# Layer 1's input projection in eight pairs over both streams, seven block products for each pair

## The chip, the cores and the metric

The program runs on one core of a Trainium2 chip, in one launch. The metric is the device time of one execution in microseconds (us). Six queues of instructions matter: TensorE (PE in the rows; its weight loads are PEld), VectorE (DVE), ScalarE (ACT), GpSimd (POOL), and SyncE (SP) and ACT also issue DMAs. Each engine executes its own instructions in order and waits on semaphores for the others.

## The reference

A two-layer encoder trunk is applied to two requests ("streams") with the same weights, each of 512 tokens and 1024 channels. What the change touches is the first matmul of a layer and what reads it:

```python
h = _rmsnorm(x, norm_mix)
proj = h @ w_in
q, k, v, g, hy_in, pool_in = jnp.split(proj, [R, 2 * R, 3 * R, 4 * R, 4 * R + 3 * HY_WIDTH], axis=-1)
ret = _head_layernorm(_retention(_rope(q) * dk ** -0.5, _rope(k), v, ...), ret_gn) * silu(g)
hy_out = _hyena(hy_in, hy_short_conv, ...)      # conv of width 3, two long convolutions by FFT
pool_out = _pool_mixer(pool_in, pool_w, pool_scale)
x = x + concat([ret, hy_out, pool_out]) @ w_out
```

`w_in` has 1024 rows and 3072 columns: 512 each for q, k, v and g (four heads of 128), 768 for the Hyena group, 256 for the pooling group. After it come a gated MLP with 2816 hidden channels and a gated per-layer embedding. All arithmetic is held to float32 accuracy.

## The kernel before

**Layout.** Activations are stored transposed: a tile holds 128 channels by 512 tokens of one stream. A weight tile of the projection is 128 output columns by all 1024 input channels, that is eight blocks of 128x128. The names of the tiles are q0 to q3, k0 to k3, g0 to g3 (one for each head), hy0 to hy5, pl0 and pl1; v stands apart, as v00 to v11, because it is computed with the tokens on the partitions (`values`).

**Float32 from float16.** Each operand is split into a high and a low float16 part (`split`: ACT writes the high part, DVE or POOL the low one), and each 128x128 block takes three matmuls: high with high, high with low, low with high. So one tile of one stream is 8 x 3 = 24 matmuls of 512 columns (`mm3`). Raw weights are loaded by SP into four buffers (`wraw`), scaled and split into nine buffers (`wspl`); both streams use a split tile while it lasts.

**Normalised input.** `norm_steps` sums squares with a small matmul (cs), DVE and POOL turn it into a scale, and eight small matmuls broadcast that into a PSUM tile (rb). `h_steps` then makes eight tiles h: DVE multiplies (hn), ACT casts the high part, and the low part is a subtraction, on DVE for the even tiles and on POOL for the odd ones.

**Pairs in the MLP.** From its fourth pair of weight tiles on, the MLP already works on both streams at once (`ffn_joint`): two weight tiles, cut into two halves of their input channels, are a 2 x 2 block matrix, the two halves of h of the two streams are another, and their product is formed with seven block products instead of eight (the form of Strassen and Winograd). Each block product (`product`) is 4 x 3 = 12 matmuls. The right-hand operands are four blocks of h and four sums of them (`ffn_sums`: 16 tiles hs, made from the kept float32 tiles hn of both streams by 16 subtractions, ten of them on POOL, and 16 splits). The left-hand operands are sums of weight blocks (`piece_pair`: four subtractions on POOL, then four splits). The results come out in three PSUM banks X, Y and Z and are combined by ACT copies (r) and DVE additions. `lace` interleaves the seven products of a pair with those of the next.

**Order of the work.** PE and SP follow exactly the order in which the program emits instructions. That order comes from a small planner (`schedule`): the work is cut into Python generators ("threads": one main thread for each stream, and threads for retention heads, Hyena, pooling, filters), each step states how long it occupies PE and how long its result will take, and the planner runs whatever is ready, side threads first. The first stream's main thread may run ahead of the second by a few weight tiles (`LAG`). The order on DVE, ACT and POOL is set by the framework's scheduler. In layer 1 of the version before, stream 0 does v, then q0, k0, g0, hy0 and so on; stream 1 follows some 40 us later through the same tiles, and the steps of heads (sc, ov), Hyena (tp, sp, iv) and pooling (pq) of both streams lie between them. The projection of the mixing output (o0 to o7) follows.

## Time and profile before

| | |
|---|---|
| median of 3 runs | 2470.57 us (2466.92 to 2471.66) |
| the profiled execution | 2464.75 us, of which its span, first to last instruction, is 2463.0 us |
| PE busy | 2387.3 us, 97% of the span |
| DVE, ACT, POOL busy | 1778.7, 1034.5 and 715.4 us (72%, 42%, 29%) |
| mean granted TensorE clock | 0.989 of full speed |
| layer 1's mixing, from the second stream's rb to the first MLP tile | 1304 to 1720 us of the span |

The busy share tells which engine sets the pace on average; the rows of waits tell where PE, although busiest, had to stand still. The time of a stretch in which PE is always busy is the number of its matmuls times their spacing. [...]

### The profile page before, as it was taken

How to read it: one execution, taken by the hardware profiler on the slowest of the kernel's cores; microseconds unless marked ns; L12 is line 12 of the kernel's file. 1: busy time of each engine (PE TensorE's matmuls, PEld its weight loads, DVE VectorE, ACT ScalarE, POOL GpSimd, SP SyncE). 2: the span in 40 equal slices, each digit the busy share in tenths (PEclk: the TensorE clock that was granted, in tenths of full speed). 3: DMA queues.
4: the chain of work that ended last, by engine and by line, in shares of the span. 5: the costliest groups of instructions: out<-in, count | busy, mean ns of one | idle time of the engine just before them, and what ended most of it. 6: DMA issues, size and time to landing. Idle time of an engine off the chain costs nothing.

```text
span 2463.0 us, 30876 instructions
## 1 busy us (share of the span) xinstructions
PE 2387.3 (97%) x12024; PEld 1171.1 (48%) x12024; DVE 1778.7 (72%) x2520; ACT 1034.5 (42%) x1555; POOL 715.4 (29%) x534
## 2 busy tenths in 40 slices
PE   5999989999999999999999999999999999999997
PEld 3544654444444444444456555544444444444443
DVE  7984886868877868866575686464987786976655
ACT  5543334344534435444533343332553453544441
POOL 3222343124234233320121223520423424332011
PEclk9999999999999999999999999999999999999998
DMA  6121020330121121113232111131012112111301
GB/s 225 65 97 62 25 75 8 128 132 32 50 68 54 52 69 48 60 53 114 73 123 91 67 43 52 35 115 64 25 46 68 57 47 69 54 58 52 112 1 69
DMA packets 64363, 168.60 MB, mean 68 GB/s; under 512 B 7574, under 2 KB 13718, under 8 KB 64216
## 3 DMA queue, kind: packets, MB, share of 16 engines
q1 hardware_dynamic: 58312, 156.40, 19.2%
q10 hardware_dynamic: 5904, 10.23, 1.1%
q8 instruction: 94, 1.54, 0.3%
q14 instruction: 53, 0.43, 0.1%
HBM read 152.18 MB, written 14.42 MB: 68 GB/s over the span
## 4 chain that ended last, share of the span: by engine, by line
PE 74%; DVE 16%; issue 4%; ACT 3%; POOL 1%; DMA 1%; SPq 0%; ACTq 0%; POOLq 0%; DVEq 0%
PE fx L1169 13%; PE ex L1169 7%; PE fy L1169 7%; PE ey L1169 4%; PE fz L1169 3%; DVE wspl L171 2%; PE s L326 2%; PE s L327 2%; PE s L328 2%; PE ez L1169 2%; DVE t L174 2%; DVE conv L171 2%; PE o L327 2%; PE o L328 2%; PE o L326 2%
## 5 line engine op out<-in xcount | busy, mean ns | idle before, releaser
L1169 PEld LDWEIGHTS <-wspl 128*128 128x128 f16 x4704 | 461.1, 98 | 566.1 <-issue 13.9
L174 POOL TENSOR_TENSOR wraw<-wraw 128x512 f32<-128x512 f32 (+1 forms) x240 | 345.5, 1440 | 653.6 <-DVE wspl L171 639.5
L168 ACT ACTIVATE wspl<-wraw 128x1024 f16<-128x1024 f32 (+2 forms) x360 | 327.1, 910 | 381.6 <-POOL wraw L174 71.1
L171 DVE SCALAR_TENSOR_TENSOR wspl<-wraw,wspl 128x1024 f16<-128x1024 f32 (+2 forms) x354 | 387.7, 1096 | 84.8 <-ACT wspl L168 83.6
L1169 PE MATMUL fx<-hs,wspl 128*128 128x512 f16 x1368 | 312.3, 382 | 7.6 <-ACT r L168 7.6
L326 PEld LDWEIGHTS <-wspl 128*128 128x128 f16 x1536 | 152.3, 99 | 182.0 <-issue 8.6
L328 PEld LDWEIGHTS <-wspl 128*128 128x128 f16 x1536 | 150.7, 98 | 183.8 <-issue 4.1
L327 PEld LDWEIGHTS <-wspl 128*128 128x128 f16 x1536 | 150.7, 98 | 177.9 <-issue 4.8
L1169 PE MATMUL ex<-at,wspl 128*128 128x512 f16 x846 | 192.7, 379 | 0.0
L174 POOL TENSOR_TENSOR y<-t,mhalf 128x4 f32<-128x4 f32 x30 | 36.1, 1203 | 399.6 <-DVE t L178 388.8
L168 ACT ACTIVATE at<-conv 128x512 f16<-128x512 f32 x142 | 89.3, 629 | 145.5 <-DVE conv L174 110.8
L174 DVE TENSOR_TENSOR at<-conv,at 128x512 f16<-128x512 f32 x142 | 126.0, 888 | 26.9 <-ACT at L168 25.5
L171 DVE SCALAR_TENSOR_TENSOR conv<-r,scaled,conv 128x511 f32<-128x511 f32 x152 | 130.5, 859 | 2.1 <-ACT conv L168 0.4
L1169 PE MATMUL fx<-h,wspl 128*128 128x512 f16 x456 | 104.6, 379 | 0.0
L1169 PE MATMUL fy<-h,wspl 128*128 128x512 f16 x456 | 104.6, 379 | 0.0
L1169 PE MATMUL fy<-hs,wspl 128*128 128x512 f16 x456 | 104.6, 379 | 0.0
L1169 PE MATMUL fz<-h,wspl 128*128 128x512 f16 x456 | 104.6, 379 | 0.0
L168 ACT ACTIVATE conv<-conv 128x512 f32<-128x512 f32 x88 | 55.3, 629 | 109.5 <-DVE conv L171 108.4
L1169 PE MATMUL ey<-at,wspl 128*128 128x512 f16 x432 | 101.1, 379 | 0.0
L174 DVE TENSOR_TENSOR acc<-acc,sq 128x512 f32<-128x512 f32 x84 | 64.2, 766 | 49.7 <-ACT sq L168 48.6
L168 ACT ACTIVATE sq<-x 128x512 f32<-128x512 f32 x80 | 49.5, 624 | 117.1 <-DVE x L171 58.5
L328 PE MATMUL s<-xs,wspl 128*128 128x512 f16 x256 | 97.0, 379 | 0.0
(246 smaller groups left out, 4758.7 us busy)
## 6 DMA issues: line engine op xcount, KB each, us to landing
wraw<-in_w SPq DMA_DIRECT2D x172, 512.0 KB, 3.7
wraw<-in_w SPq DMA_DIRECT2D x48, 384.0 KB, 3.0
x<-in_x SPq DMA_DIRECT2D x32, 256.0 KB, 4.7
dec<-ddec SPq DMA_DIRECT2D x16, 448.0 KB, 4.6
wraw<-in_w SPq DMA_DIRECT2D x16, 256.0 KB, 2.6
xsp<-x ACTq DMA_DIRECT2D x16, 256.0 KB, 2.1
x<-xsp SPq DMA_DIRECT2D x16, 256.0 KB, 4.7
out_y<-out SPq DMA_DIRECT2D x16, 256.0 KB, 2.8
```

The source lines that it names most:

```text
L168: return self.nc.scalar.activation(out=out, in_=in_, func=func, **k)
L171: return self.nc.vector.scalar_tensor_tensor(out=out, in0=in0, scalar=scalar, in1=in1, op0=op0, op1=op1)
L174: return (eng or self.nc.vector).tensor_tensor(out=out, in0=in0, in1=in1, op=op)
L326: self.nc.tensor.matmul(out, wv[:, 0, kb, :], x[:, 0], start=first, stop=False)
L327: self.nc.tensor.matmul(out, wv[:, 0, kb, :], x[:, 1], start=False, stop=False)
L328: self.nc.tensor.matmul(out, wv[:, 1, kb, :], x[:, 0], start=False, stop=last)
L1169: mm = lambda a, b, start=False, stop=False: self.nc.tensor.matmul(out, a, b, start=start, stop=stop, skip_group_check=not first)
```

## The change

In layer 1 only (`TWINNED`), 16 of the 20 tiles q, k, g, hy and pl are taken as eight pairs (`TWINS`): q0 with k0, hy0 with g0, hy1 with hy2, hy3 with q1, k1 with g1, hy4 with q2, k2 with hy5, g2 with pl0. Each pair is computed for both streams together with seven block products (`mix_joint`), steps m0.0 to m7.6. The remaining four, pl1, q3, k3 and g3, follow for each stream by itself. `h_steps` keeps the float32 tiles, and `ffn_sums` makes the 16 sums when the second stream's h is there. The first stream's thread, after its v tiles, waits until the joint part is done; the second one, after its own v tiles, runs it. What follows each tile (rotation, convolution, gate, and the start of head, Hyena and pooling threads) is moved into `take`, which is called with the right stream when a result is complete. Layer 0 is as before. The core of the diff:

```diff
+TWINS = (("q0", "k0"), ("hy0", "g0"), ("hy1", "hy2"), ("hy3", "q1"), ("k1", "g1"), ("hy4", "q2"), ("k2", "hy5"), ("g2", "pl0"))
+TWINNED = (1,)
...
+        steps[4:4] = lace([f"m{i}" for i in range(len(TWINS))])
...
-            yield from self.h_steps(s, x, acc, vec[:, V_NMIX:V_NMIX + NB], h)
+            M = self.mix[l]
+            yield from self.h_steps(s, x, acc, vec[:, V_NMIX:V_NMIX + NB], h, M.hn[s] if l in TWINNED else None)
             x = None
+            M.h[s] = h
+            if s == 1 and l in TWINNED:
+                self.ffn_sums(M)
...
+                if l in TWINNED and not M.done.owner and s == 1:
+                    M.done.owner = self
+                    yield [self.decay_ev[l]]
+                    yield from self.mix_joint(l, M)
+                    M.done.set(self.clock)
+                    yield 0.0, 0.0
+                elif l in TWINNED and M.done.time is None:
+                    yield [M.done]
...
+            p = st["XYZXYXX"[q]]
+            self.product(p, w, right[q], q < 3)
+            i, s, box = 0, 0, []
+            if q in (0, 1, 3):
+                r = st[("r1", "r5", None, "r2")[q]] = self.g(name="r")
+                self.act(r, p)
+                r = None
+            elif q == 6:
+                i, box = 1, [p]
+                del state[key]
+            else:
+                n = {2: "r1", 4: "r2", 5: "r5"}[q]
+                self.tt(st[n], p, st[n], ALU.add)
+                i, s, box = int(q == 5), int(q > 2), [st.pop(n)]
+                if q < 5:
+                    del st["Z" if q == 2 else "Y"]
```

In the emitted PE order, nothing differs up to the second stream's rb of layer 1, nor from the second stream's first MLP tile on. Behind the joint part, the seven-product chain of the last pair ends with its sixth and seventh product in a row, both into bank X, with a DVE addition that reads X after the sixth.

PE, right behind the second stream's rb in layer 1. Before, the first stream's q0 follows (it reads h of the first stream, made 20 us earlier):

```order
L751 LDWEIGHTS rr2_10734
L751 MATMUL rb_10861<-identr_91,rr2_10734 128x128
L326 LDWEIGHTS wspl_10737
L326 MATMUL q0_10914<-h_10488,wspl_10737 128x512 [waits Activation_49]
L327 LDWEIGHTS wspl_10737
```

Now the second stream's v tiles follow (vp), which read the h tiles (h_10862 and on) that are made from this very rb:

```order
L762 LDWEIGHTS rr2_10734
L762 MATMUL rb_10851<-identr_91,rr2_10734 128x128
L342 LDWEIGHTS h_10862 [waits Activation_49]
L342 MATMUL vp_10964<-wspl_10230,h_10862 128x256
L343 LDWEIGHTS h_10862
L343 MATMUL vp_10964<-wspl_10230,h_10862 128x256
L344 LDWEIGHTS h_10862 [waits DVE_49]
L344 MATMUL vp_10964<-wspl_10230,h_10862 128x256
L342 LDWEIGHTS h_10867 [waits Activation_49]
```

The two tiles of q0 and k0 that stood between rb and the second stream's v are gone from there; four blocks of v now stand in a row.

POOL at the same place. Before, the second stream's four low parts of h follow one another:

```order
L174 TENSOR_TENSOR h<-hn,h 128x512 x4
L174 TENSOR_TENSOR y<-t,mhalf 128x4
L174 TENSOR_TENSOR h<-hn,h 128x512 x4
L174 TENSOR_TENSOR sw<-sw,rope 128x512
L174 TENSOR_TENSOR rt<-rt,sw 128x512
```

Now the subtractions for the sums (hn<-hn) are mixed in:

```order
L185 TENSOR_TENSOR h<-hn,h 128x512 x4
L185 TENSOR_TENSOR y<-t,mhalf 128x4
L185 TENSOR_TENSOR hn<-hn 128x512
L185 TENSOR_TENSOR h<-hn,h 128x512
L185 TENSOR_TENSOR hn<-hn 128x512
L185 TENSOR_TENSOR h<-hn,h 128x512
L185 TENSOR_TENSOR hn<-hn 128x512 x2
L185 TENSOR_TENSOR h<-hn,h 128x512
L185 TENSOR_TENSOR hn<-hn 128x512 x3
L185 TENSOR_TENSOR h<-hn,h 128x512
L185 TENSOR_TENSOR hn<-hn 128x512 x3
```

Behind y, the last low part of h (tile 7) moved from fourth to eleventh place; seven subtractions stand ahead of it.

DVE, in the first stream's Hyena step between the inverse transform (iv, on PE) and the next transposes (tp, on PE, which read abs). Before:

```order
L171 SCALAR_TENSOR_TENSOR conv_11793<-hy0_11768,scaled1_192,conv_11793 128x511 [waits DVE_49]
L174 TENSOR_TENSOR rt_11830<-k1_11797,rope_10910 128x512 [waits PE_49,Activation_49]
L174 TENSOR_TENSOR qk_11834<-rt_11830,qk_11834 128x512 [waits Activation_49]
L171 SCALAR_TENSOR_TENSOR yv_11864<-iv_11837,qs_11862 128x256 [waits Activation_49]
L171 SCALAR_TENSOR_TENSOR yv_11864<-iv_11837,qs_11862 128x256
L174 TENSOR_TENSOR yv_11864<-yv_11864,conv_11477 128x512 [waits DVE_49]
```

Now:

```order
L185 TENSOR_TENSOR r_12141<-my_11970,r_12141 128x512 [waits Activation_49]
L182 SCALAR_TENSOR_TENSOR conv_12125<-mx_11508,scaled1_192,conv_12125 128x511 [waits DVE_49]
L182 SCALAR_TENSOR_TENSOR conv_12159<-r_12141,scaled1_192,conv_12159 128x511 [waits Activation_49]
L185 TENSOR_TENSOR r_11983<-mx_11765,r_11983 128x512 [waits PE_49]
L182 SCALAR_TENSOR_TENSOR conv_12159<-r_12141,scaled1_192,conv_12159 128x511 [waits DVE_49]
L182 SCALAR_TENSOR_TENSOR wspl_12433<-wraw_11623,wspl_12433 128x1024 [waits Activation_49]
L182 SCALAR_TENSOR_TENSOR yv_12190<-iv_12163,qs_12188 128x256 [waits DVE_49]
L182 SCALAR_TENSOR_TENSOR yv_12190<-iv_12163,qs_12188 128x256
L185 TENSOR_TENSOR yv_12190<-yv_12190,conv_12125 128x512 [waits DVE_49]
```

The addition r_11983 reads bank X of the pair hy3, q1 after its sixth product, which PE executes behind iv and two more products; it now stands ahead of the reading of iv. For the second stream's iv it is the addition after the third product of the pair k1, g1.

## Rows read from the trace of the kernel before

**Rows 1.** The page, busy time by engine: busy us (share of the span), instructions.
```profile
PE 2387.3 (97%) x12024; PEld 1171.1 (48%) x12024; DVE 1778.7 (72%) x2520; ACT 1034.5 (42%) x1555; POOL 715.4 (29%) x534
```
**Rows 2.** Windows, layer 1's mixing: length, busy us of each engine, granted clock, DMA share, GB/s.
```profile
1304.00:1720.00 416.00, 413.66 (x2335) 223.51 (x2333) 259.18 (x403) 152.16 (x232) 112.92 (x95) 1.00 0.20 69
```
**Rows 3.** PE's waits in the same stretch: us in total, times, longest.
```profile
PE cs L741 <- ACT sq L168: 2.3, 2, 1.7
```
**Rows 4.** Timeline of PE, second stream's rb: start us, duration us, instruction [idle before].
```profile
1303.70 0.61 PE L751 MATMUL rb<-identr,rr 128*128 128x128 f16 x8
1304.14 0.38 PE L326 MATMUL q<-h,wspl 128*128 128x512 f16 x1
1314.50 0.27 PE L331 MATMUL vp<-wspl,h 128*128 128x256 f16 x1
1319.74 0.38 PE L326 MATMUL g<-h,wspl 128*128 128x512 f16 x1
```
**Rows 5.** Timeline of POOL there: the second stream's first and last low part of h.
```profile
1308.42 1.16 POOL L174 TENSOR_TENSOR h<-hn,h 128x512 f16<-128x512 f32 x1 [13.78 <-ACT h L168]
...
1314.55 1.15 POOL L174 TENSOR_TENSOR h<-hn,h 128x512 f16<-128x512 f32 x1 [1.01 <-ACT h L168]
```
**Rows 6.** Timeline of POOL, second stream, MLP of layer 1: subtractions mixed with low parts.
```profile
1739.63 1.27 POOL L174 TENSOR_TENSOR hn<-hn 128x512 f32<-128x512 f32 x1 [9.44 <-DVE hn L171]
...
1751.09 5.06 POOL L174 TENSOR_TENSOR hn<-hn 128x512 f32<-128x512 f32 x3
1756.11 1.60 POOL L174 TENSOR_TENSOR h<-hn,h 128x512 f16<-128x512 f32 x1
```
**Rows 7.** Timeline of PE there: rb, and the MLP tile that reads h.
```profile
1736.17 0.61 PE L751 MATMUL rb<-identr,rr 128*128 128x128 f16 x8
...
1757.76 0.38 PE L327 MATMUL fg<-h,wspl 128*128 128x512 f16 x1 [0.69 <-POOL h L174]
```
**Rows 8.** Windows behind idle stretches of PE (columns as in rows 2).
```profile
626.50:630.80 4.30, 4.23 (x12) 1.60 (x12) 3.85 (x5) 1.63 (x4) 2.40 (x2) 0.60 0.00 0
47.50:54.00 6.50, 6.44 (x31) 5.10 (x32) 6.27 (x15) 2.70 (x4) 1.39 (x1) 0.51 0.76 258
...
1283.00:1286.20 3.20, 3.20 (x17) 2.25 (x17) 2.47 (x5) 1.11 (x2) 0.00 (x0) 0.52 0.98 354
```
**Rows 9.** Timeline of PE: the wait ahead of the first, and two shorter waits.
```profile
626.57 3.74 PE L1169 MATMUL fx<-hs,wspl 128*128 128x512 f16 x10 [3.83 <-ACT r L168]
...
1282.89 0.40 PE L333 MATMUL vp<-wspl,h 128*128 128x256 f16 x1 [1.36 <-POOL h L174]
...
1617.96 1.05 PE L741 MATMUL cs<-ones,sq 128*128 128x1 f32 x8 [1.71 <-ACT sq L168]
```
**Rows 10.** DVE groups of 1300 to 1660: busy us, mean ns of one, idle before.
```profile
L171 DVE SCALAR_TENSOR_TENSOR wspl<-wraw,wspl 128x1024 f16<-128x1024 f32 x24 | 30.0, 1250 | 16.4 <-ACT wspl L168 16.2
L171 DVE SCALAR_TENSOR_TENSOR conv<-hy,scaled,conv 128x511 f32<-128x511 f32 x24 | 17.9, 745 | 10.5 <-ACT conv L168 10.3
```
**Rows 11.** Tile r in the MLP of layer 1: one addition, duration min/median/max ns.
```profile
L174 DVE TENSOR_TENSOR r<-fz,r x1: 683/683/683, 1794.8 to 1794.8; 128x512 f32<-128x512 f32 x1
```
**Rows 12.** Timeline of DVE: first and last step between an iv and its tp.
```profile
1410.95 0.74 DVE L171 SCALAR_TENSOR_TENSOR yv<-iv,qs 128x256 f32<-128x256 f32 x2
...
1417.60 0.69 DVE L174 TENSOR_TENSOR abs<-ab,abs 128x512 f16<-128x512 f32 x1 [0.16 <-ACT abs L168]
```
**Rows 13.** Timeline of PE there: what follows that iv, and the tp.
```profile
1410.25 0.38 PE L331 MATMUL sc<-qk 128*128 128x512 f16 x1
...
1423.20 1.06 PE L602 MATMUL tp<-ident,abs 128*128 128x128 f16 x16
```
**Rows 14.** Timeline of PE: sc and ov of the stage's last head.
```profile
1628.81 0.38 PE L331 MATMUL sc<-qk 128*128 128x512 f16 x1
...
1637.03 0.38 PE L331 MATMUL ov<-pt,v 128*128 128x512 f16 x1
```
**Rows 15.** Timeline of DVE: the last pt of that head.
```profile
1635.34 0.69 DVE L174 TENSOR_TENSOR pt<-st,pt 128x512 f16<-128x512 f32 x1 [0.16 <-ACT pt L168]
```

More of the change, by code (lines that the diff above doesn't have):

```diff
@@ L121, in tile_order @@
     more = ["p0", "p1"] + [f"s{m}" for m in range(NB)]
-    return tiles + more, steps + more
+    return tiles + more, steps + more, mixing
 def step_time(name):
@@ L926, in main_thread @@
-            h = None
+                box = [self._proj(l, name, h, s)]
+                yield from self.take(l, s, name, box, M, 5.15)
+            h = M.h[s] = None
             if s == 1:
                 self.rope = None
+            mix, done = M.mix[s], M.ends[s]
             yield done
@@ L1025, in main_thread, with take @@
             nc.sync.dma_start(out=io["y"][s, m], in_=t)
+    def take(self, l, s, name, box, M, cost):
+        nc, io = self.nc, self.io
+        p = box.pop()
+        if name[:2] == "hy":
+            if not M.loaded:
+                M.loaded = True
+                self.load_dft(l)
+            j = int(name[2])
+            M.hy[s][j] = self.conv3(p, self.hcw[l], j, 6)
+            p = None
+            yield cost, 0.0
+            M.hev[s][j].set(self.clock + 3.0)
+            if j == 0:
+                M.ends[s].append(Event())
+                self.spawn(self.hyena_thread(l, M.hy[s], M.hev[s], M.mix[s], M.ends[s][-1]))
+        elif name[:2] == "pl":
+            b = int(name[2])
+            if b == 0:
+                M.pw[s] = self.g(name="poolw")
+                self.load(M.pw[s][:, 0:256], io["poolw"][l])
+            rc = self.g(name="rc")
+            self.load(rc, io["rcnt"][b])
+            m = self.pooling(p, b, rc)
+            rc = p = None
+            yield cost, 0.0
+            M.ends[s].append(Event())
+            self.spawn(self.pool_thread(l, b, m, None, M.pw[s][:, b * 128:(b + 1) * 128], M.mix[s], M.ends[s][-1]))
+        elif name[0] in "qk":
+            M.qk[s].setdefault(int(name[1]), {})[name[0]] = self.rotate(p)
+            p = None
+            yield cost, 0.0
+        else:
+            hd = int(name[1])
+            sg = self.g(name="sg")
+            self.act(sg, p, ACTF.Sigmoid, scale=1.0 / WS)
+            self.stt(sg, p, 1.0 / WS, sg, ALU.mult, ALU.mult)
+            p = None
+            if hd == 0 and self.decay_ev[l].time is None:
+                yield [self.decay_ev[l]]
+            dec = self.dp.tile([128, 896], F32, tag="dec", name="dec")
+            nc.sync.dma_start(out=dec, in_=self.ddec[l, hd])
+            yield cost, 0.0
+            M.ends[s].append(Event())
+            self.spawn(self.head_thread(l, hd, M.qk[s].pop(hd), M.v[s], sg, dec, M.mix[s], M.ends[s][-1]))
@@ new lines, in mix_joint @@
+    def mix_joint(self, l, M):
+        right = self.rights(M)
+        state = {}
+        self.load_rope()
+        for _, name in STEPS[STEP_AT[l, "m0.0"]:STEP_AT[l, f"m{len(TWINS) - 1}.6"] + 1]:
+            key, q = name.split(".")
+            q = int(q)
+            w = self.weight(l, name, 0, 1)
+            st = state.setdefault(key, {})
+            if q in (0, 1, 2):
+                st["XYZ"[q]] = self.bank(name="m" + "xyz"[q])
+            p = st["XYZXYXX"[q]]
[8 more added lines that the diff above has]
+                del state[key]
+            else:
+                n = {2: "r1", 4: "r2", 5: "r5"}[q]
[3 more added lines that the diff above has]
+                    del st["Z" if q == 2 else "Y"]
+            st = p = None
+            if box:
+                yield from self.take(l, s, TWINS[int(key[1:])][i], box, M, 2.58)
+            else:
+                yield 2.58, 0.0
@@ L1229, in run @@
         self.ffn = [Ffn() for _ in range(self.depth)]
+        self.mix = [Mix() for _ in range(self.depth)]
         a = self.spawn(self.main_thread(0))
@@ L1252, in run, with __init__ @@
         self.schedule([a, b])
+class Mix:
+    def __init__(self):
+        self.h, self.hn, self.sums = [None, None], [[], []], None
+        self.mix = [[None] * NB for _ in range(2)]
+        self.hy, self.v, self.ends, self.qk, self.pw = [[None] * 6 for _ in range(2)], [[], []], [[], []], [{}, {}], [None, None]
+        self.hev = [[Event() for _ in range(6)] for _ in range(2)]
+        self.done, self.loaded = Event(), False
 class Ffn:
```

103 lines of the change are left out of this document (34 added, 69 removed).

## The prediction

> **What bounds the kernel now.** I read the page's busy times first. PE works in 97% of the span, and no other engine is above 72% [rows 1]. Then the stretch that the change touches, 1304 to 1720 us: PE is busy for 413.7 of 416 us, at the full granted clock, while DVE is busy for 259.2 (62%), ACT for 152.2 and POOL for 112.9 [rows 2]. PE's waits there come to 2.3 us in two places [rows 3]. So this stretch is as long as its matmuls. Fewer matmuls shorten it one for one, as long as PE gets its operands in time; and there is hardly any idle time to win beside them. The question is which new waits PE gets.
>
> The sum is made against the profiled execution's span of 2463.0 us. Its device time of 2464.75 us lies 5.8 us under the median of 2470.57 us; I add the difference to the median.
>
> **The matmuls.** In the timeline q0 and k0, 48 matmuls of 512 columns, take from 1304.14 to 1314.50 us [rows 4], so one takes 0.2158 us. A pair had 2 tiles x 2 streams x 24 = 96 of them and has 7 x 12 = 84 now. Eight pairs save 96 matmuls: **-20.7 us**. All of it lies on PE's path.
>
> **The second stream's v behind its own rb.** Before, q0 and k0 of the first stream stood between rb and v: rb ends at 1304.31 (1303.70 + 0.61), v starts at 1314.50 [rows 4], POOL finishes the last low part of h at 1315.70 [rows 5], and v, which walks the eight tiles in order for its first half, never waited. Now v is next to rb, and no other work of PE is put there: the first stream waits for the joint part, and its head, Hyena and pooling threads don't exist yet. So PE waits for tile 7 of h, whatever that costs. Besides, POOL now has seven subtractions for the sums ahead of that tile's low part.
>
> The same mixture exists in the MLP, where the second stream's sums are made: rb ends at 1736.78 (1736.17 + 0.61) [rows 7], POOL starts on the first subtraction at 1739.63, three subtractions in a row take 5.06 us, and the last low part ends at 1757.71 [rows 6]. That is 20.9 us behind rb. PE had other tiles to do there and still waited 0.69 us [rows 7]. With 20.9 us, tile 7 is ready at 1325.2. Of a v block (5.24 us [rows 4]) the last matmul of the first half (0.11) and the whole second half (2.62) are left then, so the block ends at 1327.95 instead of 1309.38: **+18.6 us**. The lower bound is the row without sums, 1315.70 [rows 5]: the block would end at 1318.45, +9.1. I take the upper row, because its sequence of eleven POOL operations is the one that stands here now; DVE is also busy in that time, with hn, the low parts and the first sums.
>
> POOL's low part took 1.16 us where no sums were made [rows 5] and 1.60 us amid them, and its subtraction grew from 1.27 to 1.69 us (5.06 / 3) [rows 6]. [...]
>
> With POOL at its undisturbed 1.16 and 1.27 us throughout, the eleven operations (four low parts, seven subtractions) would need 13.5 us; begun 4 us behind rb, they would end at 1321.8, and the wait would be 15.2 us.
>
> The other sums hide: the 16 low parts on DVE and 16 casts on ACT fall under the three remaining v blocks and the first products, 15.7 + 2.6 us behind the wait; the first product that reads a sum is the second of m0.
>
> **The clock behind that wait.** [...] At the start, after a longer stop, 6.44 us of work ran at 0.51 [rows 8], a loss of 3.2 us. Here PE stands for about 4 us and then does three matmuls for each tile that arrives. I take **+2.5 us**, between 1.7 and 3.2.
>
> **The end of the joint part.** The last pair's sixth and seventh product write bank X in a row, and DVE must read X in between: a matmul's tail beyond its spacing (0.38 - 0.22 [rows 4]), the addition of 0.68 [rows 11] and two hand-overs: **+1.0 us**, and up to 2.7 if the clock falls after it.
>
> **The last head.** Behind it the second stream's last head has sc, one pooling matmul, rb and then ov, about 3.9 us from the start of sc to ov; before it was 8.2 us (1628.81 to 1637.03 [rows 14]), and the last pt was done at 1636.03 [rows 15], 7.2 us after the start of sc. ov needs that pt for its last quarter, 1.9 us in; 7.2 - 5.8 is about **+1.2 us**. The wait of cs on ACT's square, 1.71 us [rows 9] of the 2.3 [rows 3], hung on the order before; those 2.3 us are taken off (**-2.3**), and **+1.0** is put in for such waits in the new order (0 to 2.3).
>
> **Hyena between iv and tp.** Both streams now pass through Hyena side by side. From iv to the last abs DVE took from 1410.95 to 1418.29, 7.3 us with one foreign instruction of 0.6 in it [rows 12], and PE came to tp 12.95 us behind iv's end (1410.25 to 1423.20 [rows 13]). Now the first stream's tp comes 13.45 us behind iv's end (an rb, two products, the other stream's iv, one product: 0.44 + 5.18 + 5.24 + 2.59). But DVE has the addition of m3's sixth product ahead of it, which is ready 5.6 us behind iv. From there: addition 0.68 [rows 11], convolution 0.75, a weight's low part 1.25 [rows 10], then 6.7 and one rotation 0.7, that is 15.7 us: 2.2 us late. For the second stream it is the addition of m4's third product, 6.1 us behind iv; then 0.68, 1.25, a low part of 0.69 [rows 12] and 6.7 + 1.4, that is 16.8 against 13.9 us: 2.9 us late. Together **+5.1 us**. No row shows this wait itself, so its bounds are 0 (if ACT or the scheduler's order gives DVE time earlier; a gain is excluded, since PE doesn't wait at these places now) and 8 (each of some 15 instructions stretched by 0.2 beside POOL's weight sums). A wait of 1.36 us [rows 9] was followed by 3.2 us at a granted clock of 0.52 [rows 8], a loss of 1.5 us; I count one such fall behind these waits, **+1.7 us** (0 to 3.4).
>
> **What hides.** DVE gets 16 low parts (0.69 [rows 12]), 6 subtractions and 24 additions (0.68 [rows 11]), and for each pair one and a half more weight splits (1.25 [rows 10]): 11 + 20 + 15 = 46 us on its 259 in a stretch of 416, three quarters busy on average and not the bound. POOL's 32 weight sums (1.3 to 1.7 us, as its other subtractions [rows 6]) come to some 50 us on 113, ACT's 16 casts, 24 copies and splits to less than 40 on 152. SP issues the same loads, moved with their tiles; the Hyena matrices are asked for when hy0 is complete, and about 40 us of PE's work lie between that and their first reader. If that cover were gone, a product would wait for a landing; nothing in the rows puts one there.
>
> **Sum.** -20.7 + 18.6 + 2.5 + 1.0 + 1.2 - 2.3 + 1.0 + 5.1 + 1.7 = **+8.1 us**, that is 2478.7 us for the median. With all low ends: -20.7 + 9.1 + 1.7 + 1.0 + 0 - 2.3 + 0 + 0 + 0 = -11.2; with all high ends about -20.7 + 18.6 + 3.2 + 2.7 + 2.5 - 0 + 0 + 8 + 3.4 = +17.7.
>
> **The rivals.** *The sums don't hold up v* (0.20): POOL comes to tile 7 earlier, as in rows 5, and the wait is 9 to 14 us. For it: DVE has no convolutions here, as it has in the MLP; against it: the emitted POOL order. With 9.1 us the whole is -1.4 us, with the Hyena waits gone too -8.2. It ends on the faster side; the point from which it decides is a wait of v under 10.5 us with the rest as summed, that is, tile 7 ready within 12.7 us of rb. *Hyena isn't late* (0.25): DVE gets through in time; +1.3 us, no change. *DVE becomes the bound in the joint part* (0.08): additions, spectra and splits pile up, the banks X are read late, and products wait in many places; +13 to +18 us. That the matmuls aren't saved is excluded by their count in the emitted order; that PE isn't the bound by rows 2.
>
> **How the numbers follow.** The forecast, all terms near the values taken, has 0.47 and its own range is +3 to +16 us. A measurement of this kernel can tell about 0.2%, 4.9 us, from no change. Faster by more: 0.12 of the first rival and 0.03 of the second, 0.15. Slower by more: 0.40 of the forecast, 0.02 of the second rival, the third with 0.08, so 0.50. Within: 0.35. The range goes from -6.6 us (the first rival with one Hyena wait left) to +16.4: 2464 to 2487 us.
>
> **What would show it.** In the changed profile: 96 fewer matmuls; behind the second stream's rb of layer 1 a v block of about 24 us in place of 5.2, with waits on POOL's and DVE's h, and a lower granted clock just behind; tile 7's low part 21 us behind rb; a wait of 1 us between the last two products; waits of tp on DVE's abs in the joint part; the MLP unchanged. The forecast is wrong if tile 7 comes within 15 us of rb, or if tp doesn't wait; it is far off if products wait for banks all through.

## The result

| | before | after |
|---|---|---|
| median | 2467.65 us (5 runs, 2466.92 to 2471.66) | 2531.78 us (5 runs, 2531.06 to 2535.04) |
| profiled span | 2463.0 us | 2530.0 us |
| ratio | | 1.0265, 95% interval 1.0254 to 1.0276 |

The changed kernel is 64 us slower. The forecast was 8 us slower, with a range up to 2487 us, so the time lies far outside of it.

The page of the changed kernel, busy time by engine, to be held against [rows 1]:

```profile
PE 2386.3 (94%) x11928; PEld 1166.3 (46%) x11928; DVE 1848.3 (73%) x2582; ACT 1067.9 (42%) x1611; POOL 781.1 (31%) x576
```

There are 96 matmuls fewer (12024 to 11928), as said. PE's busy time hardly fell (2387.3 to 2386.3), since part of the work ran at a lower clock. The windows of the mixing stretch show both losses; the columns are length, busy us (instructions) of PE, PEld, DVE, ACT and POOL, granted clock (as a share of full speed), DMA share, GB/s. Before, [rows 2] had PE busy for 413.7 of 416 us at clock 1.00:

```profile
1304.00:1330.00 26.00, 10.51 (x61) 6.21 (x60) 23.82 (x25) 8.83 (x15) 18.64 (x12) 0.61 0.00 1
1330.00:1640.00 310.00, 263.89 (x1518) 148.46 (x1517) 226.96 (x335) 131.46 (x204) 113.47 (x88) 0.93 0.19 64
1640.00:1787.00 147.00, 141.28 (x680) 67.16 (x679) 76.38 (x107) 45.81 (x70) 40.59 (x33) 0.98 0.22 75
```

No engine is the bound in the joint part: DVE, the fullest beside PE, works for 227 of 310 us, 73%. PE's waits from the second stream's rb to the first MLP tile (total us, times, longest), where before there were two waits of 2.3 us [rows 3]:

```profile
PE sp L342 <- ACT u L179: 23.0, 5, 11.3
PE mx L1235 <- ACT r L179: 13.9, 3, 7.5
PE vp L344 <- POOL h L185: 11.3, 4, 5.1
PE cs L752 <- ACT sq L179: 5.4, 1, 5.4
PE vp L342 <- ACT h L179: 2.6, 1, 2.6
PE tp L613 <- DVE abs L185: 1.8, 4, 0.8
PE ov L343 <- DVE pt L185: 1.6, 3, 0.9
PE vp L344 <- DVE h L185: 1.6, 1, 1.6
PE tp L613 <- ACT abs L179: 1.6, 1, 1.6
```

With five smaller ones (4.1 us) they come to 66.9 us. The account of the spans: +67.0 = -20.7 (matmuls) - 2.3 (the old waits) + 66.9 (new waits) + 23.1 left over. Of that rest 2.0 us lie ahead of the stretch, where PE's order is the same in both kernels (the second stream's rb starts at 1303.70 before and at 1305.67 now). The other 21 us are mostly the clock; an estimate from the three windows, 10.51 x 0.39 + 263.89 x 0.07 + 141.28 x 0.02, gives 25 us of busy time beyond what full speed needs.

**The wait of v came as forecast.** POOL there, against [rows 5]: seven subtractions for the sums now stand among the four low parts; the last of them are

```profile
1320.71 5.05 POOL L185 TENSOR_TENSOR hn<-hn 128x512 f32<-128x512 f32 x3
1325.72 1.59 POOL L185 TENSOR_TENSOR h<-hn,h 128x512 f16<-128x512 f32 x1
```

And PE at rb, and at the matmul that reads tile 7:

```profile
1305.67 0.61 PE L762 MATMUL rb<-identr,rr 128*128 128x128 f16 x8
...
1327.37 0.40 PE L344 MATMUL vp<-wspl,h 128*128 128x256 f16 x1 [5.10 <-POOL h L185]
```

Tile 7 is ready at 1327.31, 21.0 us behind the end of rb (1306.28); the forecast had 20.9. The waits of this block come to 15.5 us (the rows of vp above), and the lower clock of the first window costs about 4.1 more (10.51 x 0.39): 19.6 us, where the forecast had 18.6 + 2.5.

**The large waits are not where they were forecast.** On PE, the last 12 of the 24 matmuls of the first row are the fourth product of the second pair, which completes bank X for the copy r; the second row is the sixth product, which writes X next and waits for that copy.

```profile
1377.01 5.34 PE L1235 MATMUL mx<-hs,wspl 128*128 128x512 f16 x24
...
1395.59 4.12 PE L1235 MATMUL mx<-hs,wspl 128*128 128x512 f16 x12 [7.51 <-ACT r L179]
```

ACT at that time:

```profile
1394.42 0.63 ACT L179 ACTIVATE qk<-rt 128x512 f16<-128x512 f32 x1 [4.89 <-POOL rt L185]
1394.96 0.58 ACT L179 ACTIVATE r<-mx 128x512 f32<-128x512 f32 x1
```

POOL at that time:

```profile
1384.01 6.16 POOL L185 TENSOR_TENSOR wraw<-wraw 128x512 f32<-128x512 f32 x4 [2.47 <-DVE wspl L182]
1390.14 1.70 POOL L185 TENSOR_TENSOR sw<-sw,rope 128x512 f32<-128x512 f32 x1
1393.13 1.26 POOL L185 TENSOR_TENSOR rt<-rt,sw 128x512 f32<-128x512 f32 x1 [1.29 <-DVE rt L185]
```

Read backwards: the bank was complete at 1382.4 (1377.01 + 5.34), and the copy takes 0.58 us. It stands in ACT's queue behind the cast qk, which waits for a rotation, which waits on POOL behind four weight sums. ACT itself did nothing for 4.89 us. In these rows ACT took the two in the order in which they stand in its queue: r ran at 1394.96, 12.6 us after its bank was complete.

The longest wait, in the Hyena step of the first stream. PE:

```profile
1489.09 0.90 PE L613 MATMUL tp<-ident,abs 128*128 128x128 f16 x13 [0.44 <-DVE abs L185]
...
1506.52 0.37 PE L342 MATMUL sp<-u,fwd 128*128 128x256 f16 x1 [11.34 <-ACT u L179]
```

ACT:

```profile
1500.24 0.63 ACT L179 ACTIVATE abs<-ab 128x512 f16<-128x512 f32 x1 [4.40 <-DVE ab L185]
1500.77 0.37 ACT L179 ACTIVATE qs<-iv 128x256 f32<-128x256 f32 x1
1504.44 0.63 ACT L179 ACTIVATE abs<-ab 128x512 f16<-128x512 f32 x1 [3.30 <-DVE ab L185]
1504.97 0.58 ACT L179 ACTIVATE r<-my 128x512 f32<-128x512 f32 x1
1505.45 1.93 ACT L179 ACTIVATE u<-tp 128x1024 f16<-128x1024 f16 x2
```

tp is done at 1490, but u, the copy of its result, runs at 1505: two casts abs of the other stream stand ahead of it, and each waits for DVE. The chain behind the second abs begins with the second qs, a read of iv, which itself stands behind the first abs.

The queue is only a part of this wait. A tile is written into one of 72 general buffers, and it can't be written before the last reader of the buffer's old tile is done (in e5, below, ACT stood idle for 9.37 us ahead of a u until such a reader was done). By the addresses in the emitted program, the first of the two u goes to the place of a tile yv of the other stream. DVE's ab reads that yv until 1500.20 (its row, 1497.43 + 2.77, is shown in the last section). So u had its result at 1489.6 but no place until 1500.2; the 5.2 us from there to 1505.45 are the queue. Of the sp wait of 8.18 us, too, only 1.5 are the queue: that u had its buffer 11.2 us behind tp. The buffers of the copies r and of sq that PE waited for were free in time, so their waits are the queue's alone.

The wait of cs (5.41 us at 1656.41) is such a one: its square sq stands behind a qk that waited 9.65 us for POOL:

```profile
1654.72 0.63 ACT L179 ACTIVATE qk<-rt 128x512 f16<-128x512 f32 x1 [9.65 <-POOL rt L185]
```

### The profile page after: what moved, and what is told of

Same layout as the page of the kernel before. It is cut to its first block, busy times and chain, and to the rows that moved or that the text cites. A ratio compares the mean times of both kernels' runs of the same rounds, so it can differ in the third digit from the quotient of the medians.

```text
span 2530.0 us, 30902 instructions
## 1 busy us (share of the span) xinstructions
PE 2386.3 (94%) x11928; PEld 1166.3 (46%) x11928; DVE 1848.3 (73%) x2582; ACT 1067.9 (42%) x1611; POOL 781.1 (31%) x576
## 4 chain that ended last, share of the span: by engine, by line
PE 65%; DVE 18%; issue 7%; POOL 5%; ACT 4%; DMA 1%; SPq 0%; POOLq 0%; ACTq 0%; DVEq 0%
PE fx L1235 13%; PE ex L1235 7%; PE fy L1235 6%; PE ey L1235 4%; PE fz L1235 3%; DVE wspl L182 2%; DVE t L185 2%; DVE conv L182 2%; PE ez L1235 2%; PE o L338 2%; PE s L337 2%; PE s L339 2%; PE o L339 2%; PE o L337 2%; PE s L338 2%
## 5 line engine op out<-in xcount | busy, mean ns | idle before, releaser
L185 POOL TENSOR_TENSOR wraw<-wraw 128x512 f32<-128x512 f32 (+1 forms) x272 | 391.1, 1438 | 708.8 <-DVE wspl L182 693.0
L179 ACT ACTIVATE wspl<-wraw 128x1024 f16<-128x1024 f32 (+2 forms) x376 | 340.4, 907 | 405.8 <-POOL wraw L185 78.6
L182 DVE SCALAR_TENSOR_TENSOR wspl<-wraw,wspl 128x1024 f16<-128x1024 f32 (+2 forms) x370 | 406.6, 1099 | 86.3 <-ACT wspl L179 85.1
L182 DVE SCALAR_TENSOR_TENSOR conv<-r,scaled,conv 128x511 f32<-128x511 f32 x172 | 146.2, 850 | 3.2 <-ACT conv L179 1.2
```

Of the source, the lines that this page charges most:

```text
L179: return self.nc.scalar.activation(out=out, in_=in_, func=func, **k)
L182: return self.nc.vector.scalar_tensor_tensor(out=out, in0=in0, scalar=scalar, in1=in1, op0=op0, op1=op1)
L185: return (eng or self.nc.vector).tensor_tensor(out=out, in0=in0, in1=in1, op=op)
```

## The experiments

The theory that the runs were made for: **PE waits for copies by ACT (r, u, sq) that were ready, because ACT's fixed order puts casts ahead of them (qk, abs, yt) that end chains through POOL and DVE.** For r and sq the rows above bear it out; for u it is half of it. Rivals: POOL is simply late; DVE is short; two Hyena threads side by side need more room whatever the order; the joint form has a loss of its own. A further rival, that the 72 general buffers are too few, was not tested by itself: no run changes their number alone. Times below are medians; each was timed beside runs of the kernel before on the same chip (2465.6 to 2467.3 us), and the ratio is to these.

### One cause at a time

**e1.** Weight sums on DVE.

```diff
-names, gq = self.raw_names(j), None if j == f"f{PLAIN}" else self.nc.gpsimd
+names, gq = self.raw_names(j), None if j == f"f{PLAIN}" or j[0] == "m" else self.nc.gpsimd
```

> The changed kernel with one edit: the 32 weight sums of the eight joint pairs on DVE in place of POOL (about 1.55 us each on POOL in groups of four, 0.68 on DVE). Theory A, POOL is late: ACT's cast qk waited 4.89 us for a rotation that stood behind four weight sums, and the copy r behind it held up a product for 7.51 us; DVE's ab of the Hyena step was stretched to 2.77 us beside four weight sums, ahead of the wait of 11.34 us. Then those two waits shrink to under 2 and under 7 us, and the time falls by 9 to 20 us, to 2512 to 2523. Rival B, ACT's fixed order is what hurts whatever POOL does: under 5 us better. Rival C, DVE is what is short in the joint part: 22 us more for it make the kernel slower by 5 to 15 us.

2523.55 us (1.0217 to 1.0248), 8 us better, just short of the range expected. The wait of 7.51 shrank to 4.59, that of 11.34 only to 10.27. POOL's sums are a part, not the cause.

**e2.** Rotations on DVE.

```diff
-self.tt(sw, sw, self.rope[1], ALU.mult, self.nc.gpsimd)
-self.tt(t, t, sw, ALU.add, self.nc.gpsimd)
+self.tt(sw, sw, self.rope[1], ALU.mult, eng or self.nc.gpsimd)     # eng: DVE in layer 1
+self.tt(t, t, sw, ALU.add, eng or self.nc.gpsimd)
```

> The changed kernel with one edit: the two POOL operations of each rotation of layer 1 (product with the sine table and addition, 16 rotations) on DVE. Theory A: every long wait of ACT's qk was for POOL's rt; without POOL in that chain the copies r and the squares sq behind qk come in time, so that the product waits of 7.5 and 2.7 us and the wait of cs of 5.4 us go, with the lower clock behind them: 12 to 20 us better, 2512 to 2520. Rival C, DVE is short: 22 us more work on it cost as much as is won or more, 2528 to 2545. The Hyena waits of 23 us stay under both.

2518.7 us (1.0197 to 1.0229), 13 us better: products for r 6.5 us, cs 2.3 us, sp still 20.2 us. Both edits give DVE 32 more instructions of some 0.68 us, 22 us in all (its measured busy time rose by 7.3 and 23.2 us), and gain, so DVE isn't short (that rival falls here).

**e3.** More room for the Hyena steps in PE's order.

```diff
+WIDE = {"fold": (0.0, 10), "tok": (0.9, 12), "spec": (0, 18), "inv": (0, 16)}
-        yield LAT["tok"]
+        yield lat["tok"]      # WIDE in layer 1, and so for fold, spec, inv
```

> The changed kernel with wider due times for the Hyena steps of layer 1 in the planner (fold 10 for 7, transposes 12 for 4, spectra 18 for 14, inverse 16 for 11 us), so that PE does more products between a Hyena step and its successor; 75 general buffers for 72, which the longer lives need. Theory: the 23 us in which sp waits for ACT's copies u are there because the two streams' Hyena steps run side by side and u stands behind the other stream's steps on ACT; with 8 us more of products ahead of sp most of the 11.3 and 8.2 is covered: sp waits under 6 us, 20 to 28 us better with the clock, 2504 to 2512. Rival: what delays u delays the copies r as well, and the products put in between wait instead: under 8 us better.

2528.26 us (1.0238 to 1.0272), 3.5 us better, a miss. PE's waits show why:

```profile
PE mx L1237 <- ACT r L180: 24.7, 4, 10.3
...
PE my L1237 <- ACT r L180: 8.5, 2, 7.3
```

sp no longer waits for u, but the products put in its place wait for r: 14 us became 33. Room before a Hyena step alone doesn't end the loss. What holds these r is again both things: by the program's addresses the r behind the two longest waits (10.30 and 7.26 us) had their buffers only 20.2 and 16.6 us behind their products, when DVE had read the old tiles, and stood 5.9 and 3.1 us more in ACT's queue. This was with 75 buffers.

**e4.** The four unpaired tiles ahead of the joint part.

```diff
-steps[4:4] = lace([f"m{i}" for i in range(len(TWINS))])
+steps[8:8] = lace([f"m{i}" for i in range(len(TWINS))])   # pl1, q3, k3, g3 come first
```

> The changed kernel with the four tiles that are not paired (pl1, q3, k3, g3) done ahead of the joint part in place of behind it, by both streams: the first stream's four tiles, 20.7 us of matmuls, then stand between the second stream's rb and its v; 75 general buffers for 72. Theory: the wait of v for h tile 7 (14.9 us, and 3.5 us of lower clock) goes, 15 to 18 us better; the head and pooling steps of the last pair then end the part, whose waits grow by some 4 us: 2513 to 2520 in all. Rival: DVE and ACT are still busy with the sums when the products begin, and the products wait instead: under 6 us better.

2530.08 us (1.0248 to 1.0278), 1.7 us better, a miss. The waits of v went from 15.5 to 4.4 us, but cs for sq grew to 9.2, sp to 25.6, and pq and ov waited 9.9 us (ov 3.1 before this edit).

**e5.** The Hyena casts abs and yt by DVE.

```diff
-        self.act(hi, src, scale=scale)
+        if own:                        # fold and spectrum of layer 1
+            self.nc.vector.tensor_copy(hi, src)
+        else:
+            self.act(hi, src, scale=scale)
```

> The changed kernel with one edit: in layer 1's Hyena the high-part casts abs and yt are written by DVE in place of ACT, so that ACT no longer stands in the chain iv, yv, ab, abs or in the spectra. Theory: the 23 us in which sp waits for ACT's copies u are there because u stands in ACT's queue behind abs and yt of the other stream, each of which waits for DVE (4.40, 3.30, 2.63 us); with these casts gone from ACT the copies u run when tp is done, sp waits under 8 us, and the kernel is 15 to 28 us faster, 2503 to 2516. Rival, the DVE side of the chain is what takes the time: 24 casts more on DVE (16 us) delay tp and the additions as much as is won, 2522 to 2540.

2538.23 us (1.0277 to 1.0308), 6 us slower, a miss. sp waited 17.8 us in place of 23.0, but tp 6.8 in place of 3.4 and ov, for pt, 5.0 in place of 1.6. Taking the casts off ACT isn't the cure. Here the buffers show by themselves: no cast abs or yt stands ahead of u on ACT, which is idle, tp is done at 1440.4, and u, which reads nothing but tp, still waits for DVE's yt, a reader of its buffer's old tile:

```profile
1448.78 1.94 ACT L179 ACTIVATE u<-tp 128x1024 f16<-128x1024 f16 x2 [9.37 <-DVE yt L185]
```

**e6.** e1, e2 and e5 together.

> The changed kernel with the three edits of this study on queues together: weight sums on DVE, the rotations' POOL operations on DVE, the Hyena casts on DVE. If the losses are queues standing behind late strangers, the three add up: 8 + 13 + 15 to 28 us, of which some 5 us are counted twice, gives 2490 to 2505, and of the 67 us of waits and clock the 15 us of v's wait and some 15 in small waits stay. If DVE is short (60 us more work in some 300, 73% busy now), it is slower than the best of the three single edits, over 2515.

2507.7 us (1.0153 to 1.0184), 24 us better; sp 14.9, products for r 3.5, cs 2.3 us. It is a little short of the range expected: e1 and e2 alone add up to 21 us, so e5 adds little here too.

**e9.** The order of the casts. A cast qk, abs or yt is written into the program when the planner's clock says that its input is there, and behind the latest r, u or sq. The expectation calls this another order on ACT alone, but the edit moves the whole split: the low part moves in DVE's order too, and with both the time at which their input's buffer comes free.

```diff
-        self.split(r[:, 0], r[:, 1], t)
+        self.later(2.6 + 3.5, r, t)         # abs: 2.6 + 2.5; yt: 3.3 + 1.3 * pr
...
+    def flush(self, at=0.0, tiles=()):      # after every step, and ahead of a reader
...
+                with self.tc.issue_after(self.latest):
+                    fn()
```

> The changed kernel with another order on ACT alone: from the joint part on, the casts qk, abs and yt, which end chains through POOL and DVE, are written into the program only when the planner's clock says that their input will be there, and then behind the latest copy r, copy u or square sq on ACT. No work moves to another engine, PE's and SP's order is the same, the buffers are 72. Theory: the losses of the joint part are copies that were ready but stood in ACT's queue behind casts that were not; the waits of sp for u (23.0 us), of products for r (14.3) and of cs for sq (5.4) together fall from 43 to under 20 us, and the time by 20 to 35 us with the clock, 2497 to 2512. Rival: the chains themselves are too long for the room that PE's order gives them; then the casts come later still, tp and sc wait in their place, and the time changes by less than 8 us.

2497.22 us (1.0115 to 1.0145): 34.6 us better, more than half of the loss, with not one operation moved to another engine and with the same 72 buffers. PE's waits:

```profile
PE tp L637 <- ACT abs L179: 7.8, 4, 4.1
PE sp L366 <- ACT u L179: 6.2, 3, 4.2
PE mx L1263 <- ACT r L179: 3.5, 2, 2.7
```

The waits for u, r and sq fell from 42.7 to 9.7 us. The price is that tp now waits for abs (for ACT's half 7.8 us in place of 1.6, for DVE's 3.2 in place of 1.8). DVE had stood in front of its low parts qk for 31.3 us, waiting for ACT's casts; now for 8.3. How much of the gain is ACT's order and how much DVE's, no run tells apart. At the place of the longest wait, tp is done at 1480.56 and ACT does u at 1486.26, 5.7 us behind it in place of 15.5, and sp waits 1.57 us:

```profile
1479.23 0.79 ACT L179 ACTIVATE qs<-iv 128x256 f32<-128x256 f32 x2
...
1484.67 0.61 ACT L179 ACTIVATE abs<-ab 128x512 f16<-128x512 f32 x1
1485.19 0.58 ACT L179 ACTIVATE r<-my 128x512 f32<-128x512 f32 x1
1485.72 0.63 ACT L179 ACTIVATE abs<-ab 128x512 f16<-128x512 f32 x1
1486.26 1.92 ACT L179 ACTIVATE u<-tp 128x1024 f16<-128x1024 f16 x2
```

The two abs still stand ahead of u. What changed is that both qs, which read iv, now run together ahead of them, so DVE gets its inputs early, abs comes early, and u's buffer is free 3.6 us behind tp in place of 10.7.

**e12.** The subtractions of the sums behind h's low parts, on POOL and on DVE.

```diff
-                self.ffn_sums(M)
+                with self.tc.issue_after(self.lows[0]), self.tc.issue_after(self.lows[1]):
+                    self.ffn_sums(M)
```

> The changed kernel with one edit: the 16 subtractions for the sums of h are queued behind the last low parts of h on POOL and on DVE. The prediction's term for v by itself. If the sums on POOL set it, tile 7 comes at the row of before, 11 to 12 us behind rb in place of 21.0; v's waits fall from 14.9 to 4 to 6 us, and the time by 8 to 12 us, if the first product that reads a sum still has it in time (18 us of v blocks and one product lie between). If DVE's own work is what makes tile 7 late, the wait stays over 10 us. If the later sums hold up the first products, the gain is under 4 us.

2529.67 us (1.0241 to 1.0269), 2 us better. The waits of v fell to 5.5 us (tile 7 came 11.8 us behind rb; the row of the prediction's lower bound has 11.4), but the first pair's product then waited:

```profile
1354.12 5.28 PE L1239 MATMUL mx<-hs,wspl 128*128 128x512 f16 x12 [8.30 <-ACT r L179]
```

It had waited 3.69 us there. What v gave back, half went into the next wait for r.

### Another arrangement, and all together

These runs use 75 general buffers in place of 72, as e3 and e4 did.

**e7, e8.** Four pairs, or five with their weight sums on DVE, behind the Hyena tiles.

```
e7: v q0 k0 g0 hy0..hy5 by stream | (q1,k1) (q2,k2) (g1,q3) (g2,k3) | g3 pl0 pl1 by stream
e8: v q0 hy0..hy5 by stream | (k0,g0) (q1,k1) (q2,g1) (k2,g2) (q3,k3) | g3 pl0 pl1 by stream
```

> Four pairs in place of eight, put behind the Hyena tiles: each stream does v, q0, k0, g0 and hy0 to hy5 by itself, the second one some tiles behind the first; then the pairs q1 with k1, q2 with k2, g1 with q3, g2 with k3 jointly; then g3, pl0 and pl1 by stream. The 16 sums are made three tiles ahead of the joint part. 75 general buffers for 72. It saves 48 matmuls, 10.4 us. Theory: the two streams' Hyena steps are apart again and v has q0, k0 between itself and rb, so that the waits of sp and of v are as before; rotations behind weight sums on POOL still hold up some copies r, 5 to 10 us; 2457 to 2468. Rival, the joint form itself makes the product wait for its banks in this part: four pairs lose half of what eight do, 30 us, 2480 to 2500.

> As the run with four pairs, with five: each stream does v, q0 and hy0 to hy5 by itself, then jointly k0 with g0, q1 with k1, q2 with g1, k2 with g2, q3 with k3, then g3, pl0, pl1 by stream; and the weight sums of the pairs on DVE. It saves 60 matmuls, 12.9 us. Theory: the waits that are left are a few copies r behind late rotations, 3 to 8 us, 2455 to 2465. Rival as in the run with four pairs: 2480 to 2500.

2499.03 us (1.0119 to 1.015) and 2501.39 us (1.0125 to 1.0159): the first in the rival's range, the second just above it. But not for its reason: the largest wait isn't in the joint form. In e7, where the Hyena tiles are not paired, sp still waited 9.71 us; ACT there:

```profile
1461.12 0.63 ACT L179 ACTIVATE yt<-t 128x512 f16<-128x512 f32 x1 [2.03 <-DVE t L185]
1461.65 1.92 ACT L179 ACTIVATE u<-tp 128x1024 f16<-128x1024 f16 x2
```

tp was done at 1442, but u stands behind four yt of the other stream, and its buffer was free at 1455.7 only; 6 us are the queue's. So pairing the Hyena tiles was not needed for such a wait. It is enough that the two streams' chains meet in ACT's order and in the buffers, as they do here too.

**e10, e11.** e9's order of the casts, from the start of layer 1's mixing, and e2's rotations, with the arrangement of e4 and with the five pairs of e8 (weight sums on POOL).

> Three edits that have been tried one by one, together: the four unpaired tiles ahead of the joint part (fills the time behind the second stream's rb), the ACT order of the run before from the start of layer 1's mixing on, and the rotations' POOL operations on DVE; 75 general buffers. If the causes are the ones named (v behind its own rb, ACT's queue behind late casts, POOL's rotations), what is left is some 10 us of waits at the end of the part and some 10 small ones beside 20.7 us fewer matmuls: 2462 to 2478. If PE's order leaves the chains too little room, over 2490.

> Five pairs behind the Hyena tiles as in the run with five pairs, weight sums on POOL, with the ACT order of the runs before from the start of layer 1's mixing on and the rotations on DVE. It had 11.1 us of sp waiting for u, 7.8 of cs for sq, 4.1 of products for r. With those gone and 12.9 us fewer matmuls: 2460 to 2475. If PE's order leaves the chains too little room, over 2490.

2484.91 us (1.0062 to 1.0094), over the range expected, and 2473.48 us (1.0021 to 1.004), within it. e8 and e11 differ in the order of the casts and in where rotations and weight sums are done: 28 us.

**e13, e14.** All Hyena tiles first, then five pairs; or hy0 to hy3 first and six pairs; with the edits of e9, e2 and e12.

```
e13: v hy0..hy5 by stream | (q0,k0) (q1,g0) (k1,g1) (q2,k2) (q3,g2) | k3 g3 pl0 pl1 by stream
e14: v hy0..hy3 by stream | (q0,k0) (hy4,hy5) (q1,g0) (k1,g1) (q2,k2) (q3,g2) | k3 g3 pl0 pl1 by stream
```

> All causes found so far removed at once: each stream does v and hy0 to hy5 by itself, then five pairs jointly (q0 with k0, q1 with g0, k1 with g1, q2 with k2, q3 with g2), then k3, g3, pl0, pl1 by stream; sums behind the low parts of h; casts qk, abs, yt placed on ACT by the planner's clock; rotations on DVE; 75 general buffers. It saves 60 matmuls, 12.9 us; the earlier run of this kind had 16 us of waits and 6 of clock. If the causes are complete, 6 to 12 us of waits and clock are left: 2460 to 2468, no slower than the kernel before. If the joint form brings a loss of its own that has not been named, 2470 or more.

> As the run with five pairs, with hy4 and hy5 as a sixth pair behind the first: 72 matmuls fewer, 15.5 us. Here the second half of each stream's Hyena falls into the joint part, side by side. If ACT's queue was the whole cause of the Hyena waits, it is 0 to 3 us faster than the run with five pairs, 2458 to 2466; if the Hyena chains need room of their own beside the joint products, tp and sp wait again and it is 3 to 12 us slower.

2484.14 us (1.0058 to 1.0083) and 2475.18 us (1.0023 to 1.0048), both misses; e13 lies where the rival of a loss of the joint form's own was expected. What was left were waits of tp for abs: 16.4 us in e13, 10.6 in e14. In e14 POOL's four weight sums had become

```profile
1374.70 11.98 POOL L185 TENSOR_TENSOR wraw<-wraw 128x512 f32<-128x512 f32 x4 [14.06 <-DVE wspl L182]
```

and ACT's weight cast waited for them, and another one for 2.50 us more, with the Hyena's qs behind both (it runs at 1387.67):

```profile
1383.15 1.06 ACT L179 ACTIVATE wspl<-wraw 128x1024 f16<-128x1024 f32 x1 [4.73 <-POOL wraw L185]
```

**e15, e16.** e14 with all subtractions of h and of weights on DVE and due times for fold 10, transposes 5, inverse 14 us; rotations on POOL (e15) or DVE (e16).

> The run with six pairs, with the 10 subtractions for the sums of h and all weight sums on DVE in place of POOL, the rotations on POOL again, and wider due times for two Hyena steps in the planner (fold 10 for 7, inverse 14 for 11 us). In the run before four weight sums on POOL took 11.98 us beside DVE's casts of sums, ACT's splits waited 4.73 and 2.50 us for them with the Hyena's qs and abs behind, and DVE's own subtractions took 1.7 us each beside POOL's. If that is what was left, the waits of tp (10.6 us) and of the products (3.9) fall by half or more: 2460 to 2470. If DVE is now the one that is short, it is slower than the run before, over 2476.

> As e15, with the rotations on DVE too. If a rotation on POOL, with nothing else there, comes in time, the two are the same within 3 us, 2460 to 2470, and DVE's 12 us more work cost nothing or a little; if rotations are still what the casts qk and the copies behind them wait for, this one is 3 to 8 us faster.

2475.35 us (1.0024 to 1.0051) and 2475.18 us (1.0025 to 1.005): no better than e14. With the subtractions off POOL, it doesn't matter where the rotations are. tp waited 6.6 and 6.5 us, iv 7.0 and 5.6.

**e17.** e15 with more room for the Hyena steps (its transposes had 5 us in e15, not 4).

```diff
-WIDE = {"fold": (0.0, 10), "tok": (0.9, 5), "spec": (0, 14), "inv": (0, 14)}
+WIDE = {"fold": (0.0, 11), "tok": (0.9, 6), "spec": (0, 20), "inv": (0, 18)}
```

> The run e15 with wider due times again for the Hyena steps in the planner (fold 11, transposes 6, spectra 20, inverse 18 us; e15 had 10, 4, 14 and 14). In e3 the same kind of edit moved the waits from sp to the products, since ACT's queue held copies up wherever they stood. Now that ACT's order follows the planner's clock, room before a step should end its wait: of the 13.6 us in which tp and iv wait for abs and yt in e15 8 or more go, with 2 to 3 us of clock, 2463 to 2469, level with the kernel before. If the waits move on to other steps again (products, ov, cs), it stays at 2472 to 2478.

2465.41 us (11 runs; 0.9989 to 1.0007): 10 us better than e15, and level with the kernel before. tp and iv together wait 2.4 us. The kind of edit that only moved waits about in e3 ends them here, where the order of the casts follows the planner's clock.

**e18.** The change's own arrangement, eight pairs right behind v, with all those edits: e9's order, e12, subtractions on DVE, the due times of e17.

> The changed kernel's own arrangement (eight pairs directly behind the second stream's v, the four other tiles last) with the edits of e17: casts qk, abs and yt placed on ACT by the planner's clock, subtractions and weight sums on DVE, sums of h behind the low parts, Hyena due times 11, 6, 20 and 18 us; 75 general buffers. What e12 left of v's waits (5.5 us) and the end of the part stay. If the arrangement itself costs only that, the result is 20.7 us saved less about 6 for v, 9 at the end, 5 of clock and 5 of small waits: 2463 to 2473. If putting the Hyena tiles of both streams into the joint part costs in itself, because the chains of both streams and the sums meet on DVE, tp, sp and products wait 20 us or more: 2478 to 2495.

2467.01 us (12 runs; 0.9999 to 1.0016): 65 us better than the changed kernel, level with the kernel before. The window of the whole stretch, and PE's largest waits in it:

```profile
1304.00:1720.00 416.00, 397.60 (x2229) 214.76 (x2228) 334.15 (x498) 183.29 (x284) 117.05 (x93) 0.98 0.22 74
```

```profile
PE my L1269 <- DVE t L186: 3.3, 1, 3.3
PE sp L368 <- DVE st L183: 3.3, 2, 2.9
PE ov L369 <- DVE pt L186: 2.8, 3, 1.9
```

So neither the arrangement nor the joint form carries the loss. What each of the edits gives to the 65 us, the three more buffers among them, is known for e9, e12 and the weight sums (e1) only, each by itself. DVE does 334 us of work here in place of 259 [rows 2], 80% of the stretch, and two thirds of the waits that are left (12.6 of 18.4 us) are behind DVE. None of the runs is faster than the kernel before beyond its interval: the 20.7 us that 96 matmuls give go into 18.4 us of waits (416 - 397.6) and some 5 us of lower clock behind those of v.

## Why the prediction was wrong

- *Matmuls, -20.7 us*: right; 96 fewer.
- *v behind its own rb, +18.6 and +2.5 of clock*: right. Tile 7 came at 21.0 us (20.9); 15.5 us of waits and some 4.1 of clock (the first window ran at 0.61) make 19.6 for 21.1, the clock's part above its bound of 3.2. The low bound, 1.7, is what 4.23 us of work lost at a clock of 0.60 [rows 8], behind the 3.83 us of [rows 9]. e12 confirms the row of the lower bound and the cause, but also that taking it away gains 2 us only, which no step of the prediction said: the next wait stood right behind.
- *Hyena between iv and tp, +5.1*: 3.4 us, on abs as said (1.8 for DVE's half, 1.6 for ACT's). But the sum stopped at tp. The other stream's chain holds up the copies u behind tp, by ACT's queue and by the buffers, and there it cost 23.0 us. The upper bound, 8, rests on 0.2 us for each DVE instruction beside POOL's weight sums, an assumption that no run shows; two ab there took 2.77 us in place of 0.76 (last section).
- *End of the joint part, +1.0*: 0.78 us. *Last head, +1.2*: 0.3 us. *Waits of cs, +1.0*: 5.4 us, behind a late rotation. Some 4 us more, of rb and ov at 1437 to 1440 and of ov at 1558 to 1560, had no term.
- *"What hides"*: **this is the step that failed.** ACT's 40 casts and copies were set against its idle time (152 busy of 416 us), POOL's weight sums against its 113. Both shares stayed low (186 and 173 us of 483), and yet PE waited 42.7 us for ACT's copies: a copy needs its turn in the queue and a free buffer, not idle time on average. What stands ahead of r, u and sq on ACT, and what that waits for, stands in the emitted order, which the prediction reads for DVE and POOL only; what last reads the buffer of u stands in the program too. The sum put both at nothing. e9, which mends the order, puts this step at 35 us; the buffers' share by itself is not measured.
- *Clock, 1.7 us behind the other waits*: 21 us left over in the account of the stretch, 4 of them behind the waits of v. That is some 0.3 us for each us of waiting here (21 / 66.9).
- *The third rival, DVE is the bound, 0.08, +13 to +18*: its sign, that products wait for banks, came true in a few places (14.3 us); the engine was another, and the total that it gave a quarter of the one measured. Even in e18, where DVE works for 80% of the stretch, PE works for 96% of it.
- *The range* held terms between bounds from rows, but neither a queue that holds up strangers nor a buffer that isn't free had a term, so no bound reached the time.

Open: which step of the framework's scheduling put casts so far ahead of copies. What more buffers alone would give, and which part of e9's gain is DVE's new order. e13 is 9 us slower than e14: 2.6 us are the matmuls of the pair that it lacks, 5.8 longer waits of tp for abs, and why tp waits longer there is not settled.

## What to carry to other kernels

When work is added beside a busy TensorE, don't weigh it by the other engines' idle share. For each copy or cast that PE waits for, read what stands ahead of it in its engine's order and what that waits for, and which instruction last reads the buffer that it will write. Here a short copy behind a cast that ended a chain through two other engines inherited the chain (r, 0.58 us long, came 12.6 us after its bank was complete), and so did a copy whose buffer that chain still held (u, whose result was there at 1489.6, had no place until 1500.2); the row of PE's waits names the copy's engine in both cases. More room before one reader moved such waits to another reader here (e3); it paid after the order was mended (e17).

## What was not expected of the hardware

Beside each other, POOL and DVE slowed down more than the prediction allowed. Four weight sums on POOL took 6.16 us in one place and 11.98 in another (e14), where DVE was making low parts of the sums; two of these, at 1379.35, took 1.29 us. In the changed kernel DVE's two ab took 2.77 us beside four weight sums, which began 0.55 us earlier; behind them two more of the same form took 0.76:

```profile
1497.43 2.77 DVE L185 TENSOR_TENSOR ab<-yv 128x256 f32<-128x256 f32 x2
...
1503.58 0.76 DVE L185 TENSOR_TENSOR ab<-yv 128x256 f32<-128x256 f32 x2
```

In the changed kernel DVE, which began later here, was the one slowed: these four weight sums took 6.12 us, much as in the first place. In e14 it was POOL: DVE's two low parts took 0.65 us each, no more than the 0.69 of [rows 12]. What decides between the two, no run shows.
